# One stream of half-size weight sums beside the attention heads of a hybrid encoder block, and later norms of the last head

## The chip, the cores and the metric

The kernel runs on one core of one Trainium2 chip. The metric is device time in microseconds (us) of one execution; the kernel before has a median of 1367.48 us over 3 runs (1367.04 to 1368.94).

The engines are named as in the profile: PE is TensorE's matmul and PEld its weight load, DVE is VectorE, ACT is ScalarE, POOL is GpSimd. SP is SyncE, which here issues every DMA. Each engine executes its own instructions strictly in the order of its queue; between engines there are semaphores.

## The reference, cut to what matters

One layer of a bidirectional hybrid encoder, with 1024 tokens and width 1024, in float32:

```python
h = rmsnorm(x, norm_mix)
q, k, v, r, lr_f, lr_b, u, g_a, g_b = split(h @ w_in)
# gated linear attention, 4 heads, a forward and a backward scan, summed
o = rmsnorm_per_head(gla(q, k, v, a_f) + flip(gla(flip(q, k, v, a_b)))) * gla_norm
y_a = (silu(r) * o) @ w_branch_gla
y_b = pooling_mixer(u)
x = x + (sigmoid(g_a) * y_a + sigmoid(g_b) * y_b) @ w_out
x = x + swiglu_ffn(rmsnorm(x)); return rmsnorm(x)
```

The change concerns the stretch from about 85 to 370 us: the four attention heads, the weights that are made ready beside them (`w_branch_gla`, called `w_branch` in the kernel, and the r columns of `w_in`), and the first products with r's weights.

## The kernel before, in words

**Three products for one.** A float32 matrix is split in a high part, a cast on ACT (L201), and a low part, a subtraction on POOL or DVE (L202); a product is then three matmuls of 512 columns: high by high, high by low, low by high (L273). A weight is used only after its raw block was loaded (`raw`, four buffers), cast on ACT (`wh`) and subtracted (`wl`).

**Seven products for eight.** The large products are Strassen-like: they need sums and differences of weight quadrants. For `w_branch` and r these are made ahead on POOL (`padd`, `psub`, L755), in place in the tiles that were loaded, and stored to DRAM (`s_out3/5/6/7` and `r_out0..3_3/5/6/7`, L736), to be loaded as ordinary weights later.

**The stream beside.** `beside` (L726) turns a list of jobs into steps. A step makes one sum, or issues loads, or does nothing; the store of a sum is put three steps later (`PUT = 3`). `pump` is called after each product with its cost in units (one unit is one triple product of 512 columns) and starts a step of the stream when `every` units have gone by. It also advances the attention head in work (`side`) and runs steps put off by `soon`. These stand in a first-in-first-out list: a step with a long delay holds back those that were put in behind it.

**`w_branch` before.** `branch_jobs(k)`, for k from 0 to 3, takes two slots of 128x2x512 (`wsum`), loads 512 KB into each (L597, rows of 2 KB), spends two empty steps, makes four sums of 128x512, and stores four times 256 KB; `every` is 1.6. Behind it `r_jobs` takes eight pieces of one slot each: two loads of 256 KB (L650), four sums of 128x2x128, four stores of 128 KB, with the loads of the next piece issued ahead of the sums of this one; `every` is 1.2.

**Order.** The order of instructions on each engine follows from the order in which the Python program emits them, with a scheduler that decides by which slot of the pool comes free. `slots` has 39 places of 4 KB per partition; nearly all tiles of this stretch (`wsum`, `rraw`, `qe`, `ke`, `kt`, `sb`, `o`, `trl`) take one, and a tile's first write waits for all readers, stores included, of the tile that had its place before. SP's DMAs use eight semaphores in turn, so each DMA also waits until the one eight places ahead of it has landed.

**A head.** `attention(h)` makes gated queries and keys (`qe`: ACT writes an exponential, POOL multiplies it by q, L985; `ke` on DVE), turns the keys (`kp` on PE, `kt` on ACT and DVE), runs the backward states (`st`, `so`, `sb`), the scores (`sc` on PE, L1031; masked on DVE, L1036; split in `p` on ACT and DVE), and then, in the output loop over eight chunks n, sums products into `op` and copies them to `o` (L1130). While a head's scalar work goes on, PE has products of the next weights in between. During head 1 these are the value weights of heads 2 and 3 (`ps` with `wv` and `wl`/`wh`, loads at L795). The turned outputs of finished heads go to DRAM as `o_out` (L563), eight DMAs per head.

**The last head's end.** When its output loop is done, its two `o` tiles are normalised in four parts (`norm`, two instructions at L1095 each), and these stand in the list of `soon`. In the same stretch DVE makes two low parts of feature sums (`trl`, L706), adds r's products into r (L1366), and multiplies r's rows by the loaded outputs (`ol`, L1312), after which `ob_out` is stored.

Of the kernel before, what the change touches and what calls it, by code (L numbers as in the profile page):

```python
# [17 lines left out]
P = 128  # L18
# [4 lines left out]
HALF = 512  # L23
# [31 lines left out]
def kernel(  # L55
# [20 lines left out]
    nc = tc.nc  # L76
# [524 lines left out]
            yield None, None, None  # L601


    def rows_of(w, k, left=False):
        raw = [slot(s="wsum") for _ in range(2)]
        both = w[:, :].rearrange("(i k p) (j c) -> k p i j c", i=2, p=P, j=2)[k]
        x11, x12, x21, x22 = (t[:, i, :] for t in raw for i in range(2))
        srcs = [both[:, :, i, :] if left else both[:, i, :, :] for i in range(2)]
        return (x11, x12, x21, x22), loading(srcs, [t[:, :, :] for t in raw])

    def branch_jobs(k):
        (x11, x12, x21, x22), loads = rows_of(w_branch, k, True)
        yield from loads
        for op, dst, a, b, p in (
            (padd, x22, x21, x22, 5), (psub, x21, x11, x21, 7), (psub, x11, x22, x11, 6), (psub, x12, x12, x11, 3)
        ):
            yield partial(op, dst, a, b), None, s_out[p][:, k, :]

    def output_jobs(k):
        (b11, b12, b21, b22), loads = rows_of(w_out, k)  # L620
# [18 lines left out]
    TRIO = KT // 2 - 1  # L639
    r_out = [{p: dram.tile([P, 4, P], F32, name=f"r_out{u}_{p}") for p in (3, 5, 6, 7)} for u in range(TRIO + 1)]  # L640

    def r_jobs():
        raws = {}
        todo = [(u, c) for u in range(TRIO + 1) for c in range(2)]

        def load_rows_of(u, c):
            raws[u, c] = slot(s="rraw")
            for j in range(2):
                k0, c0 = (4 * j + 2 * c) * P, R0 + 2 * u * P
                nc.sync.dma_start(  # L650
                    raws[u, c][:, j, :].rearrange("p (k x) -> p k x", k=2),
                    w_in[k0 : k0 + 2 * P, c0 : c0 + 2 * P].rearrange("(k p) x -> p k x", p=P),
                )

        yield partial(load_rows_of, *todo[0]), None, None
        for n, (u, c) in enumerate(todo):
            if n + 1 < len(todo):
                yield partial(load_rows_of, *todo[n + 1]), None, None
            halves = [raws[u, c][:, j, :].rearrange("p (k x) -> p k x", k=2) for j in range(2)]
            a11, a12, a21, a22 = (halves[j][:, :, i * P : (i + 1) * P] for i in range(2) for j in range(2))  # L660
            for op, dst, a, b, p in (
                (padd, a22, a21, a22, 5), (psub, a21, a11, a21, 7), (psub, a11, a22, a11, 6), (psub, a12, a12, a11, 3)
            ):
                yield partial(op, dst, a, b), None, r_out[u][p][:, 2 * c : 2 * c + 2, :]

    right = {}

# [245 lines left out]
    def attention(h):  # L913
# [167 lines left out]
        yield SCORES  # L1081
        while 0 not in v_tiles[h]:
            yield 0.5
        o = [slot(shape=(4, DV), s="o") for _ in range(2)]
        ms = vec(NT, "oms")
        old = sf = None
# [29 lines left out]
        for n in range(NT):  # L1116
            half, i = n // 4, n % 4
            op = bank(ps_g, "op")
            products(op[:, :DV], tokens(p, n), value(n), last=False)
            terms = []  # L1120
            if n < NT - 1:
                terms.append((chunk_of(qe, n, 1), sb[half][:, i, :]))
            if n > 0:
                terms.append((chunk_of(qe, n, 0), sf[:, :]))
            for j, (a, b) in enumerate(terms):
                if j == len(terms) - 1 and n < NT - 1:
                    sf = s1((DV,), "sf")
                    old = advance(old, n, 0, kts[half, 0], sf[:, :], n == NT - 2)
                nc.tensor.matmul(op[:, :DV], a, b, start=False, stop=j == len(terms) - 1)
            nc.vector.tensor_copy(o[half][:, i, :], op[:, :DV])  # L1130
            nc.scalar.activation(
                op[:, DV:], op[:, :DV], AF.Square, scale=1.0 / 16.0, accum_out=ms[:, n : n + 1]
            )
            if n == 0:
                yield 0.38
                kts[1, 0] = transposed_keys(1, 0)
            if n == 1:
                yield 0.75
                q_next = scores(1)
            if n == 3:  # L1140
                p = q_next
                scales[0] = rms_scale(ms[:, :4], 4, "ors")
            if h < HEADS - 1:
                if n == 5:
                    norm(0, 0)
                elif n == 6:
                    turn(0, 0)
                elif n == 7:
                    norm(0, 1)
                    turn(0, 1)  # L1150
            yield 1.02
        scales[1] = rms_scale(ms[:, 4:], 4, "ors")
        if h == HEADS - 1:
            o_heads[h] = o
            for part in range(4):
                soon(4 + 2 * part, partial(norm, part // 2, part % 2))
            return
        unscaled.extend(partial(norm_and_turn, part) for part in range(2))

# [25 lines left out]
    for h in range(HEADS):  # L1185
# [7 lines left out]
        if h == 0:  # L1193
            for ts in ((7,), (6,), (5, 4)):
                pair_products(ts)
            store_block()
            prepare_beside(map(branch_jobs, range(4)), 1.6, floor=-0.5)
            prepare_beside([r_jobs()], 1.2, floor=-0.5)
        if h == 2:
            value_weights.pop().products()  # L1200

# [1093 lines left out]
```

## Time and profile before

| what | value |
|---|---|
| median of 3 runs | 1367.48 us (1367.04 to 1368.94) |
| the profiled execution: its time | 1367.72 us |
| its span | 1365.8 us |
| mean granted TensorE clock | 0.996 |
| PE busy | 1350.0 us, 99% of the span |
| PEld, DVE, ACT, POOL busy | 82%, 62%, 48%, 59% |
| DMA, mean over the span | 196 GB/s |

The page lists the waits of each engine with what ended them ("PE ps L273 <- POOL wl L202" is: a matmul of line 273 waited for POOL's instruction of line 202). The timeline lists instructions with start, duration and, in brackets, the idle time ahead of them and its releaser. The table by windows gives each engine's busy time in a stretch, the granted clock of TensorE (PEclk, 1.00 is full), the share of time in which the DMA engines were busy, and GB/s. Times from issue to landing of DMAs are medians of a group.

### The profile page before, as it was taken

The page shows a single profiled execution, that of the slowest core. Times are in us where ns is not written, and L with a number is a line of the kernel's source. Part 1 is how long each engine was busy: PE and PEld are TensorE (multiplying, and loading weights), DVE is VectorE, ACT ScalarE, POOL GpSimd, SP SyncE. Part 2 cuts the span into 40 slices and gives each one's busy share as a digit, 9 for nine tenths or more (in the row PEclk, how much of TensorE's full clock was granted, in tenths as well). Part 3 has the DMA queues.
Part 4 walks back from the last instruction along what each step waited for, and adds up shares of the span by engine and source line. Part 5 has one row for each costly group of instructions (what it writes and reads, how often), then busy time and mean ns, then how long its engine had stood idle before and what let it go on. Part 6 is the DMA issues. An engine that isn't in the chain of part 4 may idle for free. (4 is left out here: it accounts for less than half of the span.)

```text
span 1365.8 us, 17979 instructions
## 1 busy us (share of the span) xinstructions
PE 1350.0 (99%) x6226; PEld 1122.7 (82%) x6226; DVE 851.9 (62%) x1049; ACT 651.2 (48%) x1184; POOL 809.9 (59%) x610
## 2 busy tenths in 40 slices
PE   9999899999999999999999999999999999999998
PEld 7888788888788888888888888888888888888886
DVE  6975557666345867769874855565665555343375
ACT  7375656776434445554356533333333334444253
POOL 3333748585496548658754386666666666555454
PEclk9999999999999999999999999999999999999999
DMA  7242638354997659996326354555544447975552
GB/s 228 110 162 88 181 118 236 129 157 141 299 289 243 213 187 340 382 350 229 125 78 242 126 164 155 178 178 177 177 161 139 139 140 266 390 291 185 171 215 77
DMA packets 190139, 268.24 MB, mean 196 GB/s; under 512 B 12728, under 2 KB 112608, under 8 KB 190048
## 3 DMA queue, kind: packets, MB, share of 16 engines
q1 hardware_dynamic: 189904, 266.83, 58.0%
q8 instruction: 49, 0.80, 0.2%
q14 instruction: 42, 0.34, 0.1%
q10 hardware_dynamic: 144, 0.26, 0.0%
HBM read 178.70 MB, written 88.34 MB: 196 GB/s over the span
## 5 line engine op out<-in xcount | busy, mean ns | idle before, releaser
L202 POOL TENSOR_TENSOR wl<-fs,wh 128x512 fp32r<-128x512 f32 x120 | 166.5, 1391 | 155.2 <-ACT wh L201 99.2
L273 PE MATMUL ps<-gh,wh 128*128 128x512 f32 x616 | 240.5, 390 | 0.0
L273 PE MATMUL ps<-gl,wh 128*128 128x512 f32 x616 | 239.8, 389 | 0.3 <-DVE gl L1853 0.3
L273 PE MATMUL ps<-gh,wl 128*128 128x512 f32 x616 | 239.8, 389 | 0.0
L202 POOL TENSOR_TENSOR wl<-fraw,wh 128x512 fp32r<-128x512 f32 x90 | 129.9, 1443 | 57.0 <-ACT wh L201 53.3
L202 POOL TENSOR_TENSOR ol<-gor,oh 128x1024 fp32r<-128x1024 f32 (+1 forms) x42 | 101.4, 2418 | 86.0 <-ACT oh L201 71.5
L273 PEld LDWEIGHTS ps<-gl,wh 128*128 128x128 f32 x616 | 115.7, 188 | 24.3 <-DVE gl L1853 0.7
L273 PEld LDWEIGHTS ps<-gh,wh 128*128 128x128 f32 x616 | 115.7, 188 | 24.2 <-ACT hb L1872 0.2
L273 PEld LDWEIGHTS ps<-gh,wl 128*128 128x128 f32 x616 | 115.6, 188 | 24.1
L202 POOL TENSOR_TENSOR wl<-wraw,wh 128x512 fp32r<-128x512 f32 x56 | 94.1, 1708 | 44.0 <-ACT wh L201 43.9
L273 PE MATMUL ps<-hh,wh 128*128 128x512 f32 x296 | 119.8, 405 | 0.1
L273 PE MATMUL ps<-ol,oh 128*128 128x512 f32 x308 | 119.8, 389 | 0.0
L273 PE MATMUL ps<-oh,oh 128*128 128x512 f32 x308 | 119.8, 389 | 0.0
L273 PE MATMUL ps<-oh,ol 128*128 128x512 f32 x308 | 119.8, 389 | 0.0
L273 PE MATMUL ps<-hh,wl 128*128 128x512 f32 x296 | 115.6, 391 | 0.2 <-POOL wl L202 0.2
L273 PE MATMUL ps<-hl,wh 128*128 128x512 f32 x296 | 115.5, 390 | 0.0
L202 DVE TENSOR_TENSOR ol<-wor,oh 128x1024 fp32r<-128x1024 f32 (+1 forms) x42 | 62.7, 1503 | 67.4 <-ACT oh L201 54.9
L273 PE MATMUL ps<-trh,wh 128*128 128x512 f32 x224 | 89.2, 398 | 1.2 <-DVE r L1366 0.8
L273 PE MATMUL ps<-trh,wl 128*128 128x512 f32 x224 | 87.3, 390 | 0.0
L273 PE MATMUL ps<-trl,wh 128*128 128x512 f32 x224 | 87.2, 389 | 0.0
L201 ACT CAST wh<-fs 128x512 fp32r<-128x512 f32 x120 | 73.8, 615 | 27.4 <-DVE fs L1222 22.2
L201 ACT CAST oh<-wor 128x1024 fp32r<-128x1024 f32 (+1 forms) x42 | 41.1, 978 | 63.4 <-PE ps L273 24.3
(286 smaller groups left out, 3152.7 us busy)
## 6 DMA issues: line engine op xcount, KB each, us to landing
fraw<-in_w_ffn_in_dram SPq DMA_DIRECT2D x44, 512.0 KB, 6.9
gor<-g_out SPq DMA_DIRECT2D x35, 512.0 KB, 4.6
g_out<-s SPq DMA_DIRECT2D x44, 256.0 KB, 2.3
fraw<-in_w_in_dram SPq DMA_DIRECT2D x20, 512.0 KB, 5.7
wor<-t_out SPq DMA_DIRECT2D x20, 512.0 KB, 4.4
g_out<-g SPq DMA_DIRECT2D x33, 256.0 KB, 2.5
x<-in_x_dram SPq DMA_DIRECT2D x16, 512.0 KB, 4.4
wor<-in_w_ffn_out_dram SPq DMA_DIRECT2D x15, 512.0 KB, 7.9
```

What stands on the lines that cost most here:

```text
L201: nc.scalar.copy(hi, src)
L202: eng.tensor_tensor(lo, src, as_f32(hi), op=ALU.subtract)
L273: nc.tensor.matmul(ps, a[i], b[j], start=first and n == 0, stop=last and n == 2, skip_group_check=onto)
```

## The change

The two streams become one. `sum_pieces` takes a list of pieces, each a pair of a load and a function that says where a sum goes; the loads of piece n + 1 are issued ahead of the sums of piece n. `w_branch` now comes in eight pieces (k, s) of one slot: two loads of 256 KB in rows of 1 KB, four sums of 128x256, four stores of 128 KB. r's eight pieces follow in the same list, and `every` is 1.3 for all. While `tight[0]` is true, the stream does nothing in place of a load; it is true from the point at which a head takes its two `o` tiles to the fourth chunk of its output loop. The two empty steps behind a load are gone for `w_branch`. The norms of the last head get delays of 12, 15, 18 and 21 units in place of 4, 6, 8 and 10.

```diff
-    def branch_jobs(k):
-        (x11, x12, x21, x22), loads = rows_of(w_branch, k, True)
-        yield from loads
-        for op, dst, a, b, p in (
...
-            yield partial(op, dst, a, b), None, s_out[p][:, k, :]
+    def branch_piece_of(k, s):
+        cols = slice(s * HALF // 2, (s + 1) * HALF // 2)
+        both = w_branch[:, :].rearrange("(i k p) (j c) -> k j p i c", i=2, p=P, j=2)[k]
+
+        def load():
+            raw = slot(shape=(4, HALF // 2), s="wsum")
+            for j in range(2):
+                nc.sync.dma_start(raw[:, 2 * j : 2 * j + 2, :], both[j][:, :, cols])
+            return [raw[:, n, :] for n in range(4)]
+
+        return load, lambda p: s_out[p][:, k, cols]
...
+    tight = [False]
+
+    def sum_pieces(pieces):
+        raws = []
+
+        def load(n):
+            raws.append(pieces[n][0]())
+
+        yield partial(load, 0), None, None
+        for n, (_, dst) in enumerate(pieces):
+            if n + 1 < len(pieces):
+                while tight[0]:
+                    yield None, None, None
+                yield partial(load, n + 1), None, None
+            a11, a12, a21, a22 = raws[n]
+            for op, to, a, b, p in (
                 (padd, a22, a21, a22, 5), (psub, a21, a11, a21, 7), (psub, a11, a22, a11, 6), (psub, a12, a12, a11, 3)
             ):
-                yield partial(op, dst, a, b), None, r_out[u][p][:, 2 * c : 2 * c + 2, :]
+                yield partial(op, to, a, b), None, dst(p)
...
+        tight[0] = True
         o = [slot(shape=(4, DV), s="o") for _ in range(2)]
...
             if n == 3:
+                tight[0] = False
                 p = q_next
...
-                soon(4 + 2 * part, partial(norm, part // 2, part % 2))
+                soon(12 + 3 * part, partial(norm, part // 2, part % 2))
...
-            prepare_beside(map(branch_jobs, range(4)), 1.6, floor=-0.5)
-            prepare_beside([r_jobs()], 1.2, floor=-0.5)
+            prepare_beside([sum_pieces(
+                [branch_piece_of(k, s) for k in range(4) for s in range(2)]
+                + [r_piece_of(u, c) for u in range(TRIO + 1) for c in range(2)]
+            )], 1.3, floor=-0.5)
```

PE's and ACT's instructions keep their number and order. The places where the order of the other engines changes, or what an instruction waits for, and that matter below:

POOL in front of the last two value weights of heads 2 and 3 (`wl` from `raw_280` and `raw_284` before, `raw_280` and `raw_285` now). `wsum` are the pieces of `w_branch`, `qe` and `fac` belong to head 1. Before:

```order
L755 TENSOR_TENSOR wsum_293_1643<-wsum_293_1643 128x512
L985 TENSOR_TENSOR qe_295_1665<-qe_295_1665,q_149_1042 128x512
L986 TENSOR_TENSOR fac_296_1666<-fac_296_1666 128x4
L755 TENSOR_TENSOR wsum_293_1643<-wsum_292_1642,wsum_293_1643 128x512
L755 TENSOR_TENSOR wsum_292_1642<-wsum_293_1643,wsum_292_1642 128x512
L985 TENSOR_TENSOR qe_295_1665<-qe_295_1665,q_149_1042 128x512
L986 TENSOR_TENSOR fac_300_1698<-fac_300_1698 128x4
L755 TENSOR_TENSOR wsum_292_1642<-wsum_292_1642 128x512
L202 TENSOR_TENSOR wl_305_1732<-raw_280_1579,wh_304_1731 128x512
L202 TENSOR_TENSOR wl_307_1736<-raw_284_1615,wh_306_1735 128x512
```

The same stretch of POOL now:

```order
L768 TENSOR_TENSOR wsum_232_1379<-wsum_232_1379 128x256
L768 TENSOR_TENSOR wsum_282_1600<-wsum_282_1600 128x256
L998 TENSOR_TENSOR qe_295_1685<-qe_295_1685,q_149_1042 128x512
L999 TENSOR_TENSOR fac_296_1686<-fac_296_1686 128x4
L768 TENSOR_TENSOR wsum_282_1600<-wsum_282_1600 128x256 x3
L998 TENSOR_TENSOR qe_295_1685<-qe_295_1685,q_149_1042 128x512
L999 TENSOR_TENSOR fac_300_1721<-fac_300_1721 128x4
L202 TENSOR_TENSOR wl_306_1758<-raw_280_1594,wh_305_1757 128x512
L202 TENSOR_TENSOR wl_308_1762<-raw_285_1633,wh_307_1761 128x512
L768 TENSOR_TENSOR wsum_294_1682<-wsum_294_1682 128x256 x3
L998 TENSOR_TENSOR qe_288_1642<-qe_288_1642,q_149_1042 128x512
L999 TENSOR_TENSOR fac_312_1779<-fac_312_1779 128x4
```

The two value weights have five sums of half the size ahead of them, of two pieces, in place of four whole ones; the fourth sum and the first stand in front of the first `qe`. Between `wl_308` and the last `qe` of head 1 there are three half sums of a further piece; before, that `qe` stood directly behind `wl_307`. In the same place SP's queue, before:

```order
L795 DMA raw_280_1579<-in_w_in_dram 128x512
L563 DMA o_out0_585<-ot_247_1432 32x8x128 x4
L563 DMA o_out0_585<-ot_267_1515 32x8x128 x4
L736 DMA s_out5_540<-wsum_220_1319 128x512
L795 DMA raw_284_1615<-in_w_in_dram 128x512
L736 DMA s_out7_542<-wsum_220_1319 128x512
L597 DMA wsum_292_1642<-in_w_branch_gla_dram 128x2x512
L597 DMA wsum_293_1643<-in_w_branch_gla_dram 128x2x512
```

SP's queue there now:

```order
L808 DMA raw_280_1594<-in_w_in_dram 128x512
L749 DMA s_out7_542<-wsum_188_1202 128x256
L617 DMA wsum_282_1600<-in_w_branch_gla_dram 128x2x256 x2
L563 DMA o_out0_585<-ot_247_1444 32x8x128 x4
L563 DMA o_out0_585<-ot_267_1530 32x8x128 x4
L749 DMA s_out6_541<-wsum_188_1202 128x256
L808 DMA raw_285_1633<-in_w_in_dram 128x512
```

The loads of the piece that POOL sums there have moved from behind eight `o_out` stores, a `raw` load and two more stores to the front of them; the last value weight's load has three more DMAs ahead of it.

ACT in head 1's output loop (`kt` are the turned keys of the second half, for the forward scan; `sf` and `so` are states, `p` the masked scores' high part). Before, with the semaphores that each row waits for:

```order
L1131 ACTIVATE op_352_1931,oms_350_1928<-op_352_1931 128x256 [waits DVE_49]
L201 CAST kt_358_1953<-kp_357_1948 128x512 [waits DMAHW0_49,DMAHW6_49,PE_49,Pool_49]
L1023 ACTIVATE sf_360_1965<-st_362_1970,fac_300_1698 128x256 [waits DVE_49,Activation_49]
L1023 ACTIVATE so_363_1972<-st_362_1970,fac_300_1698 128x256 [waits Activation_49]
L1131 ACTIVATE op_359_1960,oms_350_1928<-op_359_1960 128x256 [waits DVE_49]
```

ACT there now:

```order
L1145 ACTIVATE op_353_1970,oms_351_1967<-op_353_1970 128x256 [waits DVE_49]
L201 CAST kt_359_1992<-kp_358_1987 128x512 [waits PE_49]
L1036 ACTIVATE sf_361_2003<-st_363_2008,fac_300_1721 128x256 [waits DVE_49,Activation_49]
L1036 ACTIVATE so_364_2010<-st_363_2008,fac_300_1721 128x256 [waits Activation_49]
L1145 ACTIVATE op_360_1998,oms_351_1967<-op_360_1998 128x256 [waits DVE_49]
```

The order is the same, but the place in the pool of `kt` is another. Before it was that of a `w_branch` tile, whose sums and stores it waited for. Now it is the place of `ke_293`, the gated keys of the same half, whose last reader is the last of the sixteen score matmuls of that half (`sc_366`); the wait that is left, on PE, is for that matmul.

DVE behind the last head (`ps` and `r` are r's products and rows). Before:

```order
L1366 TENSOR_TENSOR r_587_3048<-ps_641_3260,r_587_3048 128x512
L706 TENSOR_TENSOR trl_705_3504<-trl_705_3504,trh_725_3595 128x1024
L706 TENSOR_TENSOR trl_706_3505<-trl_706_3505,trh_730_3623 128x1024
L1095 SCALAR_TENSOR_TENSOR o_662_3351<-o_662_3351,ors_717_3562,gain_row_664_3353 128x256 x2
L1312 TENSOR_TENSOR r_566_2956<-ol_721_3572,r_566_2956 128x512 x2
L1366 TENSOR_TENSOR r_596_3083<-ps_652_3305,r_596_3083 128x512
```

DVE there now:

```order
L1383 TENSOR_TENSOR r_587_3088<-ps_641_3300,r_587_3088 128x512
L719 TENSOR_TENSOR trl_705_3544<-trl_705_3544,trh_725_3633 128x1024
L719 TENSOR_TENSOR trl_706_3545<-trl_706_3545,trh_730_3657 128x1024
L1109 SCALAR_TENSOR_TENSOR o_661_3390<-o_661_3390,ors_696_3513,gain_row_664_3393 128x256 x2
L1383 TENSOR_TENSOR r_596_3123<-ps_652_3345,r_596_3123 128x512
```

Six norms that stood ahead of the first `trl` are now behind it, two of them ahead of `r_596`; the multiplications of r's rows by `ol` moved behind all eight norms, and with them the first stores of `ob_out`, which now stand on SP behind the loads of the blocks that follow.

More of the change, by code (lines that the diff above doesn't have):

```diff
@@ L601, in loading, with rows_of @@
             yield None, None, None
-    def rows_of(w, k, left=False):
+    def rows_of(w, k):
         raw = [slot(s="wsum") for _ in range(2)]
@@ L607, in rows_of @@
         x11, x12, x21, x22 = (t[:, i, :] for t in raw for i in range(2))
-        srcs = [both[:, :, i, :] if left else both[:, i, :, :] for i in range(2)]
-        return (x11, x12, x21, x22), loading(srcs, [t[:, :, :] for t in raw])
-    def branch_jobs(k):
-        (x11, x12, x21, x22), loads = rows_of(w_branch, k, True)
-        yield from loads
-        for op, dst, a, b, p in (
-            (padd, x22, x21, x22, 5), (psub, x21, x11, x21, 7), (psub, x11, x22, x11, 6), (psub, x12, x12, x11, 3)
-        ):
-            yield partial(op, dst, a, b), None, s_out[p][:, k, :]
+        return (x11, x12, x21, x22), loading([both[:, i, :, :] for i in range(2)], [t[:, :, :] for t in raw])
+    def branch_piece_of(k, s):
[7 more added lines that the diff above has]
+        return load, lambda p: s_out[p][:, k, cols]
     def output_jobs(k):
@@ L640, with r_piece_of, load @@
     r_out = [{p: dram.tile([P, 4, P], F32, name=f"r_out{u}_{p}") for p in (3, 5, 6, 7)} for u in range(TRIO + 1)]
[L642 to L647, printed above, removed]
+    def r_piece_of(u, c):
+        def load():
+            raw = slot(s="rraw")
             for j in range(2):
@@ L650, in load_rows_of @@
                 nc.sync.dma_start(
-                    raws[u, c][:, j, :].rearrange("p (k x) -> p k x", k=2),
+                    raw[:, j, :].rearrange("p (k x) -> p k x", k=2),
                     w_in[k0 : k0 + 2 * P, c0 : c0 + 2 * P].rearrange("(k p) x -> p k x", p=P),
                 )
[L655 to L661, printed above, removed]
+            halves = [raw[:, j, :].rearrange("p (k x) -> p k x", k=2) for j in range(2)]
+            return [halves[j][:, :, i * P : (i + 1) * P] for i in range(2) for j in range(2)]
+        return load, lambda p: r_out[u][p][:, 2 * c : 2 * c + 2, :]
+    tight = [False]
[11 more added lines that the diff above has]
+            for op, to, a, b, p in (
                 (padd, a22, a21, a22, 5), (psub, a21, a11, a21, 7), (psub, a11, a22, a11, 6), (psub, a12, a12, a11, 3)
             ):
-                yield partial(op, dst, a, b), None, r_out[u][p][:, 2 * c : 2 * c + 2, :]
+                yield partial(op, to, a, b), None, dst(p)
     right = {}
```

## The prediction

> **What bounds the kernel now.** First the waits of PE over the whole span, since PE is busy 1350.0 of 1365.8 us and only its idle time can be won.
>
> ```profile
> span 1365.8 us, 17979 instructions
> ```
>
> ```profile
> PE ps L273 <- POOL wl L202: 4.5, 3, 4.2
> PE tr L326 <- DVE xn L309: 1.5, 1, 1.5
> ...
> PE ps L273 <- DVE r L1366: 0.8, 1, 0.8
> PE ps L273 <- DVE ga L1642: 0.4, 1, 0.4
> ```
>
> One wait for a low part on POOL takes 4.2 us; two more of that kind share 0.3. The next view is PE's timeline at that wait (start, duration, idle time ahead), then the table by windows, with PEclk behind the busy times.
>
> ```profile
> 165.82 0.39 PE L273 MATMUL ps<-wh,hh 128*128 128x512 f32 x1
> 170.36 0.80 PE L273 MATMUL ps<-wl,hh 128*128 128x512 f32 x1 [4.15 <-POOL wl L202]
> ...
> 171.38 3.62 PE L1031 MATMUL sc<-qe,ke 128*128 128x128 f32 x16
> ```
>
> ```profile
> 5.00:10.00 5.00, 3.19 (x22) 2.25 (x21) 4.10 (x13) 2.83 (x9) 1.30 (x2) 1.00 0.83 233
> ...
> 166.00:168.00 2.00, 0.21 (x1) 0.00 (x0) 0.11 (x1) 0.09 (x1) 2.00 (x4) 1.00 0.89 213
> 168.00:170.00 2.00, 0.00 (x0) 0.00 (x0) 0.00 (x0) 1.22 (x3) 2.00 (x2) 0.56 0.83 229
> ...
> 172.00:174.00 2.00, 2.00 (x12) 2.00 (x11) 0.58 (x1) 0.59 (x1) 2.00 (x3) 0.50 0.21 74
> 174.00:176.00 2.00, 2.00 (x10) 1.83 (x10) 1.36 (x4) 1.25 (x3) 1.84 (x3) 0.73 0.34 131
> ```
>
> The stall costs more than its 4.15 us. A mean of 0.56 in 168 to 170 puts the fall to half speed at 168.24, 2.03 us after the last matmul ended at 166.21; a mean of 0.73 in 174 to 176 puts the return at 175.08. So PE works at half speed from 170.36 to 175.08, 4.72 us, of which 2.36 are lost: 6.5 us in all. The wait of 1.5 us at the start (5 to 10 us) left the clock at 1.00. So a wait costs itself up to 1.5 us, and from 2.03 us on about 2.4 us more.
>
> The Trainium skill, "TensorE: Matmul & The Clock Gate", Part 1, lets the clock halve after an idle window of about 3.4 us, free-running, and return after one of busy time; by that the half speed would cost 1.7 us and the stall 5.9. The row's 4.72 us at half speed decides here, and 2.03 us of idle time were enough.
>
> Why POOL was late is in its timeline, and SP's:
>
> ```profile
> 147.88 1.29 POOL L755 TENSOR_TENSOR wsum<-wsum,wsum 128x512 f32<-128x512 f32 x1
> ...
> 150.50 3.45 POOL L202 TENSOR_TENSOR wl<-raw,wh 128x512 fp32r<-128x512 f32 x2
> 153.92 1.28 POOL L985 TENSOR_TENSOR qe<-qe,q 128x512 f32<-128x512 f32 x1
> 155.16 0.19 POOL L986 TENSOR_TENSOR fac<-fac 128x4 f32<-128x4 f32 x1
> 161.17 1.29 POOL L755 TENSOR_TENSOR wsum<-wsum 128x512 f32<-128x512 f32 x1 [5.82 <-DMA wsum<-in_w_branch_gla_dram]
> ...
> 163.83 2.66 POOL L755 TENSOR_TENSOR wsum<-wsum,wsum 128x512 f32<-128x512 f32 x2
> ...
> 169.04 2.50 POOL L202 TENSOR_TENSOR wl<-raw,wh 128x512 fp32r<-128x512 f32 x2
> 171.49 1.28 POOL L985 TENSOR_TENSOR qe<-qe,q 128x512 f32<-128x512 f32 x1
> ```
>
> ```profile
> 147.09 4.69 SPq L563 DMA_DIRECT2D o_out<-ot  x8
> ...
> 152.39 0.38 SPq L795 DMA_DIRECT2D raw<-in_w_in_dram  x1
> ...
> 153.55 1.06 SPq L597 DMA_DIRECT2D wsum<-in_w_branch_gla_dram  x2
> ```
>
> The third pair of `w_branch` loads was issued at 153.55, behind eight `o_out` stores. POOL stood 5.82 us for it, and the two low parts that PE wanted lie behind those sums, at 169.04.
>
> **The change part by part.** *The pieces.* A half-size sum is shown by r's, of the same 256 elements; loads have these medians (256 KB `rraw`, 512 KB `wsum`):
>
> ```profile
> L755 POOL TENSOR_TENSOR rraw<-rraw x32: 728/738/1715, 192.8 to 245.6; 128x256 f32<-128x256 f32 x32
> ```
>
> ```profile
> rraw<-in_w_in_dram SPq DMA_DIRECT2D x16, 256.0 KB, 3.5
> ...
> s_out<-wsum SPq DMA_DIRECT2D x12, 256.0 KB, 4.3
> raw<-in_w_in_dram SPq DMA_DIRECT2D x8, 256.0 KB, 4.1
> ...
> wsum<-in_w_branch_gla_dram SPq DMA_DIRECT2D x4, 512.0 KB, 5.5
> ```
>
> I take 0.80 us for a half sum with its hand-over, so five cost 4.0 where four whole ones took 5.2. From 147.88 on POOL now does one half sum (148.7), two `wl` at the row's 3.45 (152.1), two half sums (153.7), `qe` and `fac` 1.47 (155.2), a half sum (156.0), and the first of the next piece. Its two loads now stand ahead of the `o_out` stores: issued by about 148.2 (147.09 plus a store and two issues at 0.4 to 0.5), landed at 151.7 by the 256 KB median, at 154.2 by 6.0, somewhat above the 512 KB one. POOL does not wait: half sum 156.8, `qe` and `fac` 158.3, three half sums 160.7, `qe` and `fac` 162.1, `wl` 163.4, `wl` 164.6. PE wants the first at 166.2, where its idle time begins, and the second, behind 16 scores at half of 3.62 us, near 168.4: 2.8 and 3.8 us to spare. **Term: -6.5.** POOL has slow instances (the two `wl` at 150.50 took 3.45, those at 169.04 took 2.50); two more such pairs would use 1.9 of the 2.8.
>
> *What comes late next.* The last `qe` of head 1 was done at 172.77 and led to `p`:
>
> ```profile
> 172.80 0.59 ACT L201 CAST kt<-kp 128x512 fp32r<-128x512 f32 x1 [3.58 <-POOL qe L985]
> ```
>
> ```profile
> 176.88 0.69 DVE L202 TENSOR_TENSOR p<-sc,p 128x512 fp32r<-128x512 f32 x1 [0.66 <-ACT p L201]
> ```
>
> ```profile
> 179.27 0.28 PE L273 MATMUL op<-vh,p 128*128 128x256 f32 x1
> ```
>
> `p` was ready 1.70 us before PE's use. Now three half sums come between `wl` and this `qe`: 164.6 + 2.4 + 1.28 = 168.3, 4.5 us earlier, while PE is 6.5 earlier. The cover of 1.70 falls short by 0.3. **Term: +0.3**, from 0 (fast loads, no slow sum) to 1.6 (POOL 1.3 later).
>
> *The turned keys.* Their cast on ACT now waits for the last score of the same half, and PE's next `op` takes the bank that DVE's subtraction of the cast frees:
>
> ```profile
> 183.57 1.95 PE L1031 MATMUL sc<-qe,ke 128*128 128x128 f32 x16
> ...
> 186.05 0.28 PE L273 MATMUL op<-vh,p 128*128 128x256 f32 x1
> ```
>
> ```profile
> 181.77 0.58 ACT L201 CAST kt<-kp 128x512 fp32r<-128x512 f32 x1
> ```
>
> ```profile
> 182.38 0.69 DVE L202 TENSOR_TENSOR kt<-kp,kt 128x512 fp32r<-128x512 f32 x1 [1.59 <-ACT kt L201]
> ```
>
> On these times: scores end at 185.52, cast, subtraction and three hand-overs of 0.03 add 1.36, so PE goes on at 186.88 instead of 186.05: +0.8. Behind the cast on ACT are this chunk's `sf` and `so`, behind the subtraction on DVE the state that they scale, then the masked scores and `p`; all start some 4 us later than they would, and I estimate 0.4 for the state of the chunk after, from 0 to 1.2. **Term: +1.2**, from 0.8 to 2.0. Neither reaches 2.03 us.
>
> *The norms.* On DVE the add that PE waited for stood behind six norms and two `trl`:
>
> ```profile
> 328.48 3.46 DVE L1095 SCALAR_TENSOR_TENSOR o<-o,ors,gain_row 128x256 f32<-128x256 f32 x4
> ...
> 332.46 4.36 DVE L706 TENSOR_TENSOR trl<-trl,trh 128x1024 fp32r<-128x1024 f32 x2
> ...
> 338.75 0.68 DVE L1366 TENSOR_TENSOR r<-ps,r 128x512 f32<-128x512 f32 x1
> ```
>
> It ended at 339.43, 0.8 too late, so 338.65 would have done. Now six norms are gone from ahead of the first `trl` and two stand behind the second. Even if the add ahead of the `trl` began no earlier than before, when the norms had ended at 331.9, then 0.68, 4.36, two norms 0.9 and 0.68 end at 338.5. **Term: -0.8.** The first `ob_out` stores move behind `ol` loads, which may ease or crowd the wait of 0.4 on `ga`: -0.4 to +1, I take 0. The small POOL waits (0.3 together) have one r sum less ahead: -0.2, between -0.3 and +1.
>
> *What stays hidden.* The 24 more DMAs for `w_branch` at 0.4 to 0.5 us of SP each lie beside PE.
>
> The rule on bandwidth in the Trainium skill, "DMA: Bandwidth & Descriptors", Bandwidth, speaks against pieces this small: transfers of 1 MiB and more, and in Anatomy of one DMA about 2.0 us fixed plus the bytes. By its fit half the bytes save 0.6 us of a load; the medians above, 3.5 against 5.5, show 2.0.
>
> **The sum**: -6.5 + 0.3 + 1.2 - 0.8 - 0.2 = -6.0. The profiled execution took 1367.72, 0.24 over the median of 1367.48; on the median it is **1361.5 us**. With every term at its good end (-6.5 + 0.8 - 0.8 - 0.7) it is 1360.3; with the waits at their bad ends (-6.5 + 1.6 + 2.0 - 0.8 + 1 + 1) 1365.8.
>
> **The rivals.** *The wait is exchanged.* If the last `qe` comes later than 170.1, the wait for `p` passes 2.03 us and the clock halves: 2.1 + 2.4 in place of 0.3, so 1365.7. For it: 3.45 us for two `wl`, and the loads of the next piece are behind the `o_out` stores. Against it: it takes 1.8 us more than my sum.
>
> *The loads are still late.* If the moved pair lands at 161.17 like the old one, `wl` ends at 168.5: a wait of 2.4 us and 2.4 for the clock, 4.8 instead of 6.5; `qe` then comes at 173.5 and `p` 0.7 late: -1.7 + 0.7 + 1.2 - 0.8 - 0.2, 1366.7. Against it: the pair is issued 5 us earlier and ahead of the stores that filled the DMA engines.
>
> *Slower: the last value weight.* Its load has three more DMAs ahead, and the last two `o_out` stores wait, by the eight semaphores, for the moved pair to land. Before: 152.39. Now 153.5 to 155; at 4.1 us it lands by 159.1. Its cast on ACT (0.6) and the keys' cast and subtraction behind it (1.3) make 161.0, and PE's use is:
>
> ```profile
> 161.54 0.28 PE L273 MATMUL kv<-vh,kt 128*128 128x256 f32 x1
> ```
>
> It costs from a landing at 159.6 on. If pair and load each take the 7.6 us that the old pair took (153.55 to 161.17), it lands at 164.4: a wait of 4.8, 2.4 for the clock, and `p` later by as much less what PE lost, 2 more: -6.0 + 9.2, 1370.7. Slower begins at about 163.9. By this way the rule on bandwidth in the Trainium skill, "DMA: Bandwidth & Descriptors", would hold against this change.
>
> **How the numbers follow.** Changes under 0.2% (2.7 us) can't be told from none here. Chances: forecast 0.70, exchanged wait 0.15, late loads 0.08, slower 0.07. The exchanged wait and the late loads lie around 1364.7, the bound of faster; four in ten of them I count as faster: 0.79 faster, 0.14 same, 0.07 slower. The range of 1359.3 to 1366.0 reaches 1 us under the good end, for waits after 370 us that I can't price, and takes in most of the exchanged wait.
>
> **What would show it.** Right: no PE wait on POOL `wl` near 166 and a clock of 1.00 there; POOL without a wait for `w_branch` near 155; a PE wait under 1 us for DVE `kt` behind head 1's second scores; none for `r` near 333. Wrong: PEclk under 1.00 anywhere from 100 to 370 us, or a wait for `kv` or `p` over 2 us.

## The result, and the profile after

| | kernel before | kernel after |
|---|---|---|
| median | 1367.58 us (6 runs, 1366.84 to 1368.94) | **1361.87 us** (6 runs, 1361.08 to 1362.64) |
| ratio after to before | | 0.9957, 95% interval 0.9944 to 0.9970 |
| the profiled execution: its time | 1367.72 us | 1361.08 us |
| its span | 1365.8 us | 1359.4 us |
| end of the last matmul in it | 1359.66 us | 1353.22 us |
| PE busy | 1350.0 us | 1348.2 us |

The change makes the kernel 5.7 us faster, 0.43% by the ratio, with an interval from 0.3% to 0.56%. The forecast was 1361.5 us. None of the rivals came about. All medians here are of fast executions: one, of the kernel before with late norms, took 1928.64 us at a mean granted clock of 0.659 and is left out.

The waits of PE in the kernel after (total, count, longest), without those of the start:

```profile
PE op L273 <- DVE kt L202: 0.7, 1, 0.7
PE ps L273 <- ACT ga L1654: 0.4, 1, 0.4
...
PE op L1143 <- ACT sf L1036: 0.2, 1, 0.2
PE op L273 <- DVE p L202: 0.2, 1, 0.2
...
PE ps L273 <- POOL wl L202: 0.2, 1, 0.2
```

The wait of 4.2 us for a low part is gone (the one left lies near 667 us and was there before, at 674), and so is the one for `r`. In their place stand the small ones that were forecast, for `p`, `kt` and `sf`. PE's timeline of the kernel after shows where:

```profile
165.89 0.39 PE L273 MATMUL ps<-wh,hh 128*128 128x512 f32 x1
166.12 0.39 PE L273 MATMUL ps<-wl,hh 128*128 128x512 f32 x1
...
173.40 0.38 PE L273 MATMUL op<-vh,p 128*128 128x256 f32 x1 [0.22 <-DVE p L202]
...
177.81 1.95 PE L1044 MATMUL sc<-qe,ke 128*128 128x128 f32 x16
...
181.15 0.38 PE L273 MATMUL op<-vh,p 128*128 128x256 f32 x1 [0.71 <-DVE kt L202]
181.38 0.28 PE L273 MATMUL op<-vl,p 128*128 128x256 f32 x1
```

At 166.12, where PE stood idle for 4.15 us before, the low part is there. The table by windows (PEclk is the third number from the end) has the clock at full speed where it was at half:

```profile
166.00:168.00 2.00, 2.00 (x17) 1.88 (x16) 0.00 (x0) 1.31 (x3) 1.92 (x3) 1.00 0.39 132
168.00:170.00 2.00, 2.00 (x13) 1.72 (x12) 0.81 (x2) 0.59 (x1) 2.00 (x4) 1.00 0.75 230
...
174.00:176.00 2.00, 2.00 (x15) 1.77 (x14) 1.07 (x4) 0.84 (x2) 1.51 (x3) 1.00 1.03 350
```

POOL's timeline and SP's of the kernel after, in the stretch in which POOL stood for 5.82 us before:

```profile
154.99 1.43 POOL L768 TENSOR_TENSOR wsum<-wsum 128x256 f32<-128x256 f32 x2
156.38 1.29 POOL L998 TENSOR_TENSOR qe<-qe,q 128x512 f32<-128x512 f32 x1
157.63 1.12 POOL L999 TENSOR_TENSOR fac<-fac 128x4 f32<-128x4 f32 x1
158.70 2.38 POOL L768 TENSOR_TENSOR wsum<-wsum 128x256 f32<-128x256 f32 x3
161.03 1.30 POOL L998 TENSOR_TENSOR qe<-qe,q 128x512 f32<-128x512 f32 x1
...
162.43 2.56 POOL L202 TENSOR_TENSOR wl<-raw,wh 128x512 fp32r<-128x512 f32 x2
164.93 2.38 POOL L768 TENSOR_TENSOR wsum<-wsum 128x256 f32<-128x256 f32 x3
167.26 1.27 POOL L998 TENSOR_TENSOR qe<-qe,q 128x512 f32<-128x512 f32 x1
```

```profile
147.62 1.02 SPq L617 DMA_DIRECT2D wsum<-in_w_branch_gla_dram  x2
148.69 5.34 SPq L563 DMA_DIRECT2D o_out<-ot  x8
...
154.62 0.39 SPq L808 DMA_DIRECT2D raw<-in_w_in_dram  x1
```

No row of POOL has an idle time. The pair of loads goes out at 147.62, ahead of the eight `o_out` stores, in place of 153.55 behind them. The two `wl` end at 163.7 and 165.0, the last `qe` at 168.53.

### The profile page after: what moved, and what is told of

It reads as the page before. It is cut to its first block, busy times and chain, and to the rows that moved or that the text cites. A ratio compares the mean times of both kernels' runs of the same rounds, so it can differ in the third digit from the quotient of the medians.

```text
span 1359.4 us, 18038 instructions
## 1 busy us (share of the span) xinstructions
PE 1348.2 (99%) x6226; PEld 1121.4 (82%) x6226; DVE 850.1 (63%) x1049; ACT 652.0 (48%) x1184; POOL 813.4 (60%) x626
```

## Where the 6.4 us come from

One and the same matmul starts at these times in the two profiled executions; what changes from row to row is won or lost in between:

| first matmul behind | before | after | after less before | step |
|---|---|---|---|---|
| the value products ahead of the stall | 161.54 | 161.62 | +0.08 | |
| the stall and its half speed | 175.16 | 168.59 | -6.57 | -6.65 |
| the two waits for `p` | 179.38 | 173.62 | -5.76 | +0.81 |
| those for `kt` and `sf` | 189.71 | 185.41 | -4.30 | +1.46 |
| `wl` at 226 | 226.36 | 221.60 | -4.76 | -0.46 |
| `r` at 339 | 339.81 | 333.97 | -5.84 | -1.08 |
| the waits for `ga` | 369.62 | 363.25 | -6.37 | -0.53 |

The wait of 1.5 us at the start, 0.9 in the kernel after, moves nothing behind it: the first row of the table comes behind it and differs by 0.08.

**In these traces a wait costs PE about 0.26 us more than the idle time that the profile gives for it.** PE's timeline of the kernel before has 183.57 for the scores and 186.05 and 186.18 for the two `op` behind them: 2.48 and 0.13 apart. In the kernel after the same three stand at 177.81, 181.15 and 181.38: 3.34 and 0.23 apart. That is 0.96 more, of which 0.71 is shown as idle; by their starts and durations neighbouring matmuls overlap (0.23 us from start to start at 0.39 each), and those around a wait do not. The `sf` wait of 0.23 costs 0.50 in the same way, the two waits of 0.06 and 0.22 for `p` 0.81, and the lost wait of 0.76 for `r` gave back 1.03.

## The experiments

### One pair of loads put back behind the stores

```diff
-            if n + 1 < len(pieces):
+            if n + 1 < len(pieces) and n != 3:
...
-            for op, to, a, b, p in (
+            for at, (op, to, a, b, p) in enumerate((
...
+                if n == 3 and at == 2:
+                    yield partial(load, n + 1), None, None
```

> The kernel after in which one pair of loads alone is issued two sums later: that of the fifth piece of w_branch, which on SP then stands behind the eight o_out stores and the load of the last value weight, where the kernel before had it. POOL's order, the size of the pieces and all else stay. The theory (the place in SP's queue makes the stall): the pair is issued near 154.5 us in place of 147.6, POOL stands 2 to 5 us for it near 155, low parts and the last qe come as much later, and PE waits 0.5 to 2.5 us at 166 or 1 to 3 us for p at 173: 1363.5 to 1367, with more spread. The rival (half pieces land soon enough from there too): POOL stands under 1 us and the time is that of the kernel after, 1361.9.

Measured: 1366.36 us (1364.87 to 1367.26), ratio to before 0.9988 (0.9979 to 0.9996); the kernel after, on the same chip, 1362.17. SP, POOL and PE of this kernel:

```profile
154.52 0.98 SPq L617 DMA_DIRECT2D wsum<-in_w_branch_gla_dram  x2
```

```profile
160.10 0.73 POOL L770 TENSOR_TENSOR wsum<-wsum 128x256 f32<-128x256 f32 x1 [4.09 <-DMA wsum<-in_w_branch_gla_dram]
...
165.93 2.51 POOL L202 TENSOR_TENSOR wl<-raw,wh 128x512 fp32r<-128x512 f32 x2
```

```profile
167.26 0.50 PE L273 MATMUL ps<-wl,hh 128*128 128x512 f32 x1 [0.69 <-POOL wl L202]
176.12 0.39 PE L273 MATMUL op<-vh,p 128*128 128x256 f32 x1 [2.22 <-ACT p L201]
```

Every number lies in the range of the theory: with the pieces at half size, POOL's order as in the kernel after and two DMAs moved, POOL stands 4.09 us, and the delay comes out at PE partly at `wl` and more at `p`, with a granted clock of 0.50 from 177.99 to 181.40 behind it. Of the 5.8 us that the kernel after gains on this chip (1368.01 to 1362.17), 4.2 go. A part of that is the clock: the two executions of the eleven with a mean clock of 0.999 and 1.000 took 1364.9, so without that loss the place in the queue costs about 2.7 us.

### Whole pieces, loaded one piece ahead

```diff
-        cols = slice(s * HALF // 2, (s + 1) * HALF // 2)
+        cols = slice(0, HALF)
...
-            raw = slot(shape=(4, HALF // 2), s="wsum")
+            raw = [slot(s="wsum") for _ in range(2)]
...
             prepare_beside([sum_pieces(
-                [branch_piece_of(k, s) for k in range(4) for s in range(2)]
-                + [r_piece_of(u, c) for u in range(TRIO + 1) for c in range(2)]
-            )], 1.3, floor=-0.5)
+                [branch_piece_of(k, 0) for k in range(4)]
+            )], 2.6, floor=-0.5)
+            prepare_beside([sum_pieces(
+                [r_piece_of(u, c) for u in range(TRIO + 1) for c in range(2)]
+            )], 1.3, floor=-0.5)
```

> The kernel after, but w_branch comes in four whole pieces (two loads of 512 KB into two slots, four sums of 128x512, four stores of 256 KB), loaded one piece ahead and held back by the same flag, with a step every 2.6 units; r's eight pieces are a stream of their own behind it, every 1.3. The theory (the place of the loads in SP's queue, one piece ahead and in front of the o_out stores, takes the stall away, the half size does not): no PE wait for POOL's wl near 166 us, a clock of 1.00 there, and 1361.5 to 1364, where what is above 1361.9 comes from the end of the stream near 283 to 303 us, not from 166. The rival (the half size does it, by shorter sums ahead of wl and faster landings): a wait of 2 us or more near 166 and the clock down to half behind it, 1365.5 to 1368.

Measured: 1366.29 us, ratio 0.9992 (0.9983 to 1.0001). The time lies in the rival's range and 2.3 us over the theory's, so that by the time alone the rival would seem to be right. The waits of PE say otherwise:

```profile
PE ps L273 <- ACT ga L1656: 2.2, 2, 1.2
PE kv L273 <- DVE kt L202: 2.0, 2, 1.8
...
PE op L1143 <- ACT sf L1036: 1.0, 1, 1.0
```

There is no wait for `wl` near 166 and the clock stays at 1.00; at 226 us this kernel is 4.6 us ahead of the kernel before. It gives all of that back: 4.0 at 282 to 305 us (0.25, 0.22, 1.76 and 0.22 us of idle time), and the rest with the waits for `ga` at 350 and 354. The late end of its stream should be what makes those waits. To test that, the same kernel was run with a step every 2.4 and every 1.2 units in place of 2.6 and 1.3:

> Whole pieces of w_branch, loaded one piece ahead, as in the first such kernel, but with a step every 2.4 units and r's stream every 1.2, so that the last sums of r come in time. The theory (the place of the loads alone removes the stall, and what the first such kernel lost came from the late end of its stream): no wait near 166, sf at 178 us about 1.0 as there, no waits between 283 and 305 us, 1361.5 to 1362.5. The rival (whole pieces cost more than half ones somewhere else, in POOL's longer sums or in the larger transfers): waits over 1 us that e7_half_r12 does not have, 1364 or more.

Measured: 1361.12 us (1360.30 to 1361.21), ratio 0.9952 (0.9940 to 0.9964), 0.4 us under the range, with no wait between 283 and 305 us. The `sf` wait that was expected at 178 us isn't there; in its place PE waits 0.70 us for `wl` at 166.98. So the half size isn't what removes the stall: whole pieces with their loads ahead do as well. A kernel with half pieces in the same two streams is the counterpart:

```diff
             prepare_beside([sum_pieces(
                 [branch_piece_of(k, s) for k in range(4) for s in range(2)]
-                + [r_piece_of(u, c) for u in range(TRIO + 1) for c in range(2)]
-            )], 1.3, floor=-0.5)
+            )], 1.2, floor=-0.5)
+            prepare_beside([sum_pieces(
+                [r_piece_of(u, c) for u in range(TRIO + 1) for c in range(2)]
+            )], 1.2, floor=-0.5)
```

> Half pieces as in the kernel after, in two streams of a step every 1.2 units, the second for r's sums: with the one before it a pair that differs in the size of the pieces alone. The pieces take other places in the pool, so that the second half's turned keys of head 1 do not wait for its scores. The theory: the waits for kt and sf at 181 and 185 us are gone, no waits between 283 and 305 us, 1360.5 to 1361.3, under the kernel after and within 1 us of the kernel with whole pieces. The rival: with more sums ahead of the last qe of head 1, the wait for p at 172 us grows by as much as is gained: 1361.9 or more.

Measured: 1362.80 us (1361.20 to 1364.34), ratio 0.9965 (0.9953 to 0.9977): the rival was right. The waits for `kt` and `sf` are gone, and the wait for `p` has grown from 0.06 to 1.31 us:

```profile
174.08 0.39 PE L273 MATMUL op<-vh,p 128*128 128x256 f32 x1 [1.31 <-ACT p L201]
174.81 0.41 PE L273 MATMUL op<-vh,p 128*128 128x256 f32 x1 [0.22 <-DVE p L202]
```

Last, the kernel with whole pieces once more, beside the kernel after on one chip:

> The kernel after unchanged, on the chip on which the next one is timed, so that the two can be set beside each other: 1361.5 to 1362.3.

> Whole pieces loaded one piece ahead, a step every 2.4 and every 1.2 units, unchanged, beside the kernel after. The theory that half the size gains nothing: 1360.5 to 1361.5, under the kernel after by 0.5 to 1.0, since the keys' wait at 181 us is not there and PE waits 0.7 us for wl instead. The rival, that the two differ by chance alone: within 0.3 us of each other.

Measured: the kernel after 1362.17 us (1361.18 to 1363.03), ratio 0.9959 (0.9946 to 0.9973); whole pieces **1360.36 us** (1359.89 to 1361.59), ratio 0.9946 (0.9934 to 0.9959). So a version with whole pieces is about 1.8 us faster than the kernel after in this pairing, and 1361.12 against 1361.87 from chip to chip; 0.5 to 1.0 was expected. Its PE waits by the view of waits:

```profile
PE ps L273 <- ACT ga L1656: 1.0, 1, 1.0
...
PE kv L273 <- DVE st L1029: 0.4, 1, 0.4
```

Neither `p` nor `kt` nor `sf` is waited for, nor `wl` for 0.7 as in its first execution; `st` takes 0.40 instead, at 165.43. At the matmul that starts at 189.71 in the kernel before, this kernel is 5.6 us ahead of that kernel, and the kernel after 4.3: the small waits make the difference. So the half size is not needed for the gain. That the size matters to nothing else was not shown, since the places in the pool differ between the two.

### Half pieces without the look-ahead

```diff
-        yield partial(load, 0), None, None
         for n, (_, dst) in enumerate(pieces):
-            if n + 1 < len(pieces):
-                while tight[0]:
-                    yield None, None, None
-                yield partial(load, n + 1), None, None
+            while tight[0]:
+                yield None, None, None
+            yield partial(load, n), None, None
+            for _ in range(2):
+                yield None, None, None
...
-            )], 1.3, floor=-0.5)
+            )], 0.93, floor=-0.5)
```

> The kernel after with half pieces, but each piece's loads stand directly ahead of its own sums, with two empty steps between, as the kernel before had it, and a step every 0.93 units so that the stream takes about as long. The theory: POOL waits again at its loads (2 to 6 us each), most near 155 us and again behind the heads' o_out stores, and PE waits in several places between 166 and 230 us, one of them of over 2.03 us with half speed behind it: 1366 to 1371, and most of the 5.7 us gained is gone. The rival (half pieces land in 3.5 us and two empty steps cover that, so the half size alone is enough): waits as in the kernel after, 1361.5 to 1363.

Measured: 1376.46 us, ratio 1.0064 (1.0051 to 1.0076): 5.5 us above the range that was expected, and slower than the kernel before. The rival, by which the half size alone is enough, falls. Its PE waits, and POOL behind one of r's loads:

```profile
PE ps L273 <- POOL wl L202: 9.6, 3, 8.2
PE op L273 <- DVE kt L202: 2.1, 1, 2.1
```

```profile
219.78 3.63 POOL L768 TENSOR_TENSOR rraw<-rraw 128x256 f32<-128x256 f32 x4 [7.39 <-DMA rraw<-in_w_in_dram]
```

POOL stands 7.39 us and later 3.80 for r's pieces, and the low part that PE wants at 226 lies behind them. Against the kernel after, by the starts of the same matmuls, PE loses 4.6 us up to 190 us, while POOL works on `w_branch`, and 10.6 more up to 280 us, where r's pieces lie. So the look-ahead is worth more to r's pieces than to those of `w_branch`, and the kernel before had it there already; this kernel also steps at another rate, and what that costs was not separated.

### The flag, and the place of the turned keys

Without the flag (the two lines of `while tight[0]` removed):

> The kernel after without the flag: loads are never held back. The pieces of w_branch near 150 us stand where they stood, and one of r's pieces is loaded earlier, ahead of the copies into o. The theory (the flag has no part in the gain): the waits at 172 to 185 us as in the kernel after, 1361.2 to 1362.6. The rival (loads issued while an output loop fills its o tiles make those copies wait, and PE behind them): a PE wait of over 0.5 us between 195 and 270 us that the kernel after does not have, 1363 or more.

Measured: 1362.41 us (1361.12 to 1362.75), ratio 0.9958 (0.9946 to 0.9971), the same waits at 172 to 185 us and none added between 195 and 270. The flag has no part in the gain. Set earlier, ahead of a head's first scores, it gives the pieces other places in the pool:

```diff
+        tight[0] = True
         p = scores(0)
         yield SCORES
         while 0 not in v_tiles[h]:
             yield 0.5
-        tight[0] = True
```

> The kernel after with the flag that holds loads back set ahead of the head's first scores in place of the point at which its o tiles are taken. The pieces then take other places in the pool, and the second half's turned keys no longer get the place of that half's gated keys. The theory that the kt wait at 181 us (0.71 us) and the sf wait of 0.23 behind it come from that place alone: both are gone, ACT's cast of kt does not wait for the last score of its half, and up to 270 us PE is 0.7 to 0.9 us ahead of the kernel after. Since loads are held back for longer, the stream ends later, and PE waits for its last sums near 283 to 303 us with 1.5 to 3 us in all: 1362.5 to 1364 as a whole. The rival, that the wait is one for ACT's place in the queue whatever the place in the pool: a wait of 0.6 to 0.8 for kt stays at 181 us.

Measured: 1364.38 us, ratio 0.9980 (0.9971 to 0.9989). ACT's cast of the second half's keys, in the kernel after and in this one:

```profile
179.79 0.59 ACT L201 CAST kt<-kp 128x512 fp32r<-128x512 f32 x1 [2.07 <-PE sc L1044]
```

```profile
177.03 0.56 ACT L201 CAST kt<-kp 128x512 fp32r<-128x512 f32 x1
```

The wait for the last score is gone, PE does not wait at 181 and 185, and behind 185 us it is 1.3 us ahead of the kernel after (0.7 to 0.9 was expected): the place of `ke` makes that wait, as the prediction had it. The loads are held back for longer, and PE loses 4.1 us at 281 to 304 us. The idle time there is 2.6 us in five waits, the largest 1.5 for `kt`, as expected; what each wait costs beyond its idle time brings it to 4.1 and the whole to 0.4 us over the range.

### The norms

In the kernel after, put back to `4 + 2 * part`; and in the kernel before, put to `12 + 3 * part`, each alone:

> The kernel after, with the last head's norms put back to delays of 4, 6, 8 and 10 units; nothing else is changed. By the theory of the prediction the norms are worth 0.8 us: PE's wait for DVE's r near 333 us comes back with 0.7 to 0.9 us, the wait for ga grows to 0.1 to 0.4 us more, and the time is 1362.6 to 1363.0 against 1361.9 of the kernel after. The rival, that the gap is covered by something else now that PE is 5.6 us earlier there while the norms are as early as well: 1361.9, and no wait for r. By a second rival the norms meet the ol loads and the wait for ga is the larger part: over 1363.5.

> The kernel before with the norms alone put later (delays of 12, 15, 18 and 21 units). The theory that the norms are a gain by themselves, of 0.8 us for the wait for r and about as much as undoing them cost in the kernel after (1.5 us): no wait for r near 339 us, the stall near 166 as in the kernel before, 1366.0 to 1366.7 against 1367.4 of before. The rival, that ga ends the wait anyway while PE is late: 1367.4 and the wait moved from r to ga.

Measured: 1363.34 us with early norms (ratio 0.9968, 0.9956 to 0.9980; the kernel after 0.9957), 0.3 over the range, and 1366.25 with late norms in the kernel before (0.9992, 0.9983 to 1.0001), inside it. The waits of PE with early norms:

```profile
PE ps L273 <- ACT ga L1654: 1.5, 1, 1.5
...
PE ps L273 <- DVE r L1383: 0.8, 1, 0.8
```

The wait for `r` comes back with 0.77 and goes with the late norms in the kernel before, as expected. The wait for `ga` is the part that was not expected: 1.52 us here, and 0.57 in the other. In a second profiled execution of the kernel after it was 1.01 where the first had 0.35, so its size belongs to the execution as much as to the norms. The norms are worth 1.1 to 1.5 us by the medians, which is at the edge of what can be told: the second interval reaches 1.

### The price of the exchanged wait

```diff
                 yield partial(op, to, a, b), None, dst(p)
+                for _ in range(EXTRA.get((n, p), 0)):
+                    padd(to, to, b)
+                    psub(to, to, b)
```

with `EXTRA = {(5, 7): 2}`. In this sum `b` is `to` itself, so the additions double it and the subtractions clear it: other than the expectation says, this kernel leaves out one sum of `w_branch` (product 7 of the sixth piece). POOL's four more instructions, for which the time is read, are there.

> The kernel after with four more half sums on POOL between the second low part and the last qe of head 1 (the sum of a piece is added to and taken from twice more, which gives the same value): the price of the exchanged wait of the prediction. The cover of p is used up in the kernel after, so PE waits for p 3.2 to 3.5 us at 172.7 us in any case. The clock: in the kernel with loads directly ahead it fell 2.05 us into a wait of 2.14 and 2.86 us into one of 8.16, and stayed at half for 3.41 and 10.24 us, in the kernel before for 6.83, all multiples of 3.41. The theory formed from that: the clock is set at edges 3.41 us apart, by how busy PE was between two edges; so this wait costs 3.2 to 3.5 and 1.7 or 3.4 for the clock in most executions, 1366.5 to 1368.5, spread over 1.7 us or more. The rival, that a fall needs an idle time of a whole window: 1365.0 and a clock of 1.00. By the Trainium skill, TensorE: Matmul & The Clock Gate, Part 1, an idle window of about 3.4 us is needed, which is the rival.

Measured: 1365.50 us (1363.56 to 1367.10), under the range of the theory formed and over the rival's number. PE waits 2.73 us for `p` in the profiled execution, 0.5 under what was expected. The eleven times fall in two groups: five from 1363.56 to 1364.20, with a mean granted clock of 0.999, and six from 1365.50 to 1367.10, with 0.997 and 0.998. The same program pays for a lowered clock in some executions and not in others.

The table by windows of the profiled execution, in windows that follow the clock's steps:

```profile
170.10:173.51 3.41, 2.47 (x11) 1.70 (x10) 1.08 (x2) 1.10 (x3) 3.33 (x5) 1.00 0.81 247
173.51:176.92 3.41, 1.40 (x8) 1.17 (x9) 2.73 (x7) 2.59 (x7) 3.10 (x5) 1.00 0.73 200
176.92:180.34 3.42, 3.42 (x14) 2.87 (x13) 1.20 (x4) 1.38 (x4) 1.23 (x2) 0.50 0.82 281
180.34:183.75 3.41, 3.41 (x27) 3.19 (x25) 0.00 (x0) 0.00 (x0) 0.00 (x0) 1.00 0.00 0
```

The clock falls at 176.92, when the wait (172.57 to 175.30) has been over for 1.6 us, and is back 3.41 later. The first column behind the length is PE's busy time, the second that of its weight loads (PEld). The window at half speed stands behind one in which PE was busy for 1.40 of 3.41 us. The same view of the kernel before, whose stall spans two windows, and of the half pieces in two streams, whose wait is 1.31, and of the pair put back behind the stores:

```profile
164.83:168.24 3.41, 1.38 (x8) 0.87 (x6) 0.64 (x2) 0.88 (x3) 3.33 (x5) 1.00 0.55 135
168.24:171.66 3.42, 1.30 (x4) 1.11 (x5) 0.00 (x0) 0.98 (x3) 3.42 (x4) 0.50 0.97 324
171.66:175.07 3.41, 3.41 (x17) 3.41 (x17) 1.08 (x2) 1.06 (x3) 3.33 (x4) 0.50 0.24 89
```

```profile
171.63:175.04 3.41, 1.87 (x10) 1.13 (x9) 2.12 (x6) 3.01 (x8) 3.11 (x5) 1.00 0.51 180
175.04:178.45 3.41, 3.41 (x13) 2.92 (x13) 1.85 (x6) 1.45 (x6) 0.50 (x1) 0.50 0.44 125
```

```profile
174.57:177.99 3.42, 1.64 (x10) 1.34 (x11) 2.77 (x7) 2.36 (x7) 3.19 (x5) 1.00 0.76 199
177.99:181.40 3.41, 3.41 (x14) 2.94 (x13) 0.95 (x3) 1.38 (x4) 1.00 (x2) 0.50 0.82 284
```

Two windows with 1.38 and 1.30 of busy time put two at half speed behind them, one with 1.87 and one with 1.64 put one. The rival (a whole window must be idle) falls. PE's busy time alone isn't the measure either, for a window of the first kernel with whole pieces had less than 1.87 and did not bring the clock down (it lies 83 windows of 3.413 us behind that trace's first clock record, at 6.82 us):

```profile
290.12:293.53 3.41, 1.69 (x10) 1.56 (x11) 3.07 (x7) 2.30 (x6) 3.07 (x4) 1.00 0.26 45
293.53:296.95 3.42, 3.42 (x21) 2.93 (x21) 1.06 (x3) 3.05 (x8) 1.29 (x1) 1.00 1.04 370
```

The weight loads do tell the two apart: 1.13 us of them in the window with 1.87, 1.56 in the one with 1.69. In all fourteen traces the clock fell or stayed at half behind every window of this grid with up to 1.34 us of weight loads (the pair behind the stores) and behind none with 1.44 (the flag set earlier, at 288.69 us) or more. No run changed the loads alone, so this is what goes with the fall and not yet its cause.

## Why the prediction was right, point by point

**The stall: right, -6.5 forecast, -6.65 in the profile.** The pair was issued at 147.62 (forecast 148.2), POOL did not wait, `wl` ended at 163.7 and 165.0 (163.4 and 164.6), the last value weight was issued at 154.62 (153.5 to 155). That the place in SP's queue is the cause is shown by the pair put back behind the stores; that the half size is not the cause is shown by the whole pieces loaded ahead. The prediction gave the size a part: 2.0 us earlier landings, from 3.5 and 5.5 as the medians of `rraw` and `wsum`. That step failed, and the change did not need it. The DMA issues of the kernel after have

```profile
wsum<-in_w_branch_gla_dram SPq DMA_DIRECT2D x16, 256.0 KB, 5.2
...
rraw<-in_w_in_dram SPq DMA_DIRECT2D x16, 256.0 KB, 3.4
```

Against the 5.5 of the whole pieces, half the bytes saved 0.3 us of the landing. `rraw`, of the same size, lands 1.8 sooner, and what makes it so isn't shown: it is another matrix, loaded at another time. The 0.6 that the fit of the Trainium skill gave ("DMA: Bandwidth & Descriptors", Anatomy of one DMA), a fit for DMAs that GpSimd issues where SP issues these, was nearer than the row that I took. The sum did not hang on it, as POOL needed the pair only at 155.7.

**`p`: right in its place, mis-sized.** The last `qe` ended at 168.53 (168.3), and the idle time is 0.06 and 0.22 (0.3). The cost is 0.81, by the 0.26 that each of the two waits takes beyond its idle time.

**The keys: right, 1.46 for 1.2.** 0.71 and 0.23 of idle time against 0.8 and 0.4, and 0.26 twice on top.

**The norms: right, -1.08 for -0.8**, with the same 0.26 won back. The small wait for `wl`: -0.46 for -0.2. **`ga`: taken as 0**; -0.53 in the profiled execution, and about +0.2 in the second one (1.01 and 0.26 in place of 0.13, 0.40 and twice 0.26). In eight of the eleven other profiles with late norms the last of these waits was 1.01 to 1.05 us, so the 0.35 of the profiled execution of the kernel after, the fastest of its six, is the exception.

**The sum: -6.0 forecast**, -6.4 between the ends of the last matmuls, -5.7 between the medians; the short wait for `ga` makes most of that difference. The costs were forecast 0.8 us too low in all, the gains, without `ga`, 0.7 us too low. That the two cancel, and the sum comes this near, is luck.

**The rule for the clock: wrong.** The prediction had it that a wait costs itself up to 1.5 us and 2.4 more from 2.03 us on. The 2.03 was the chance place of the stall on a grid of 3.41 us. Waits of 1.31 and 0.22 us in one window brought the clock down, and one of 1.76 did not; a fall costs about 1.7 for each window at half speed, in some executions only. The sum used the rule only to leave the small waits without a loss of clock, and there they had none; the prices of the rivals rest on it. The exchanged wait was put at 1365.7 with a wait of 2.1; the kernel with four more sums, at a wait of 2.73, has 1363.6 to 1364.2 without and 1365.5 to 1367.1 with a lowered clock, so the price holds for some executions and is 1.8 us too high for the others. The Trainium skill, "TensorE: Matmul & The Clock Gate", Part 1, has the window free-running and 3413 ns long, and the traces agree: the steps lie 3.41 us or whole multiples apart. Its condition of an idle window doesn't hold here.

**The last value weight**, the rival on the other side, was issued in the forecast range and nobody waited for it.

## What to carry to other kernels

In this kernel a load's place in the queue counted for more than its size: two DMAs moved past eight stores were worth 4.2 us by the medians, whole pieces in that place did as well as half ones, and the look-ahead of one piece is what put them there. A step that is early by the loads leaves a chain of small waits behind it (here `p`, `kt`, `sf`, `ga`), and each cost a quarter of a microsecond beyond what the profile shows as idle; where a tile's place in the pool sets such a wait, another rate of the same stream may remove it. A change that is good at its own place can be lost 120 us later, as with the first whole pieces, so the waits are compared along the whole span before a part is judged by the time.

## What the hardware showed beyond that

In these traces PE's clock changes on a grid of 3.41 us that does not follow the kernel's start: the first clock record lies from 4.34 to 7.32 us behind it. This fits the times of the kernel with four more sums, whose wait is 2.73 us: they vary from 1363.56 to 1367.10 us for one program, and the clock's mean tells the two groups apart. Behind a wait of 8.16 us in the half pieces without look-ahead the clock stayed at half for 10.24 us, three such windows.
